# Four 16-column products without a reader at nine places of a two-block transformer kernel

## The chip, the cores and the metric

The kernel runs on one core of one Trainium2 chip, and the chip's other cores do nothing. The metric is device time in microseconds for one execution, from the launch to the last output byte. A core has five engines that run on their own queues and meet only at semaphores: TensorE (PE, matrix products; its weight loads are shown as a row of their own, PEld), VectorE (DVE), ScalarE (ACT), GpSimd (POOL) and SyncE (SP), which here only issues transfers. Products are written to PSUM, a memory of eight banks; everything else lies in SBUF.

## The reference

The reference takes 256 tokens of width 1024 (float32) through a first block of two layers and then a second block of one layer. Cut to what is computed:

```python
# first block, DEPTH = 2
for layer in range(2):
    x = x + 0.5 * swiglu(rmsnorm(x, ffn1_norm[layer]), ffn1_w_gu[layer], ffn1_w_down[layer])
    h = rmsnorm(x, mix_norm[layer])
    y = mixer_gated_deltanet(h, ...) if layer == 0 else mixer_sliding_window_sinks(h, ...)
    x = x + y
    x = x + 0.5 * swiglu(rmsnorm(x, ffn2_norm[layer]), ffn2_w_gu[layer], ffn2_w_down[layer])
x = rmsnorm(x, final_norm)
# second block: 16 meta tokens are put ahead; one mixer (retention + MLA attention, two gates), one swiglu
merged = sigmoid(a_gret) * y_ret + sigmoid(a_gmla) * y_mla
x = x + merged @ w_o
x = x + swiglu(_rmsnorm(x, norm_ffn), w_gate, w_up, w_down)

def rmsnorm(x, w):   # y = x / sqrt(mean(x * x) + eps) * w
def swiglu(h, w_gu, w_down):
    gate, up = split(h @ w_gu)
    return (silu(gate) * up) @ w_down
```

The swiglu width is 2816, so each of the five feed-forward layers ("FFN" below) multiplies by 3 x 1024 x 2816 weights. With the mixers' matrices some 244 MB of weights are read once each.

## The kernel before

The activations stay in SBUF, feature-major: eight tiles of 128 features x 256 tokens (272 in the second block, with the meta tokens). Weights are streamed by `Stream`: SP loads 1 MB chunks into three buffers `raw`, and each chunk is cut into pieces of 512 columns, which ACT copies to `whi` (rounded to fp32r, L355) and DVE completes with the rest `wlo = raw - whi` (L356). Activations are split into `xh` and `xl` in the same way.

A linear layer is `lin` (L373 to L375): for each 128 x 128 weight block three products are added into one PSUM bank, whi by xh, wlo by xh and whi by xl, each with 256 moving columns. So one FFN has 44 x 8 x 3 + 8 x 22 x 3 = 1584 such products, and nearly all of the program on PE is a long run of them. Below, a *stretch* is such a run without another kind of instruction in between, and the *pitch* is the time from the start of one product to the start of the next.

Every layer starts with `opening` (L444). The norm's scale 1/rms is not needed before the first results leave PSUM, so the opening runs the first three banks (jobs a, b, c) on unscaled inputs and slips the scale in between: `rnorm_nat` sums the squares over the features by products with one moving column (L413), DVE and POOL make 1/rms of it (L426, L383), and `row_bcast` spreads it to rows of 128 partitions by two products (L435; float32, which PE runs as two passes each, so four rows in the trace). After these the rest of job c follows. There are eight openings: FFN 10, the DeltaNet mixer (whose job a is 16 columns wide), FFN 20, FFN 11, the window mixer, FFN 21, the retention mixer (272 columns) and FFN 30.

The last mixer ends with attention heads in an order written out by hand (`MLA_PLAN`), whose last entry `w3` is a product of attention weights and values (L1361). Behind it come the two gates (Stream `wga`, 16 banks by `lin`), the products with `wmo`, and the output projection `wo`.

The order of instructions on each engine is made by a list scheduler from the order of the program, priorities and its own cost estimates, so a line may be issued somewhat earlier or later than it is written. PSUM has two pools, `ps` with three banks for `lin` and `pm` with five for everything else.

Of the kernel before, what the change touches and what calls it, by code (L numbers as in the profile page):

```python
# [17 lines left out]
P = 128  # L18
D = 1024
KD = 8  # L20
S = 256
# [200 lines left out]
def kernel(ctx: ExitStack, tc: tile.TileContext, dram: dict, out: bass.AP, dump=None):  # L222
# [26 lines left out]
    pm = ctx.enter_context(tc.tile_pool(name="pm", bufs=5, space=PSUM))  # L249
    uid = [0]  # L250

    def nm(base):
        uid[0] += 1
        return f"{base}_{uid[0]}"

    def sb(at, shape, tag, dt=F32, bufs=None):

        kw = {} if bufs is None else {"bufs": bufs}
        free = int(np.prod(shape[1:]))
        whole = -(-free * 4 // LINE) * LINE // 4  # L260
        if not isinstance(at, Home):
            return at.tile(shape, dt, tag=tag, name=nm(tag), **kw)
        if at.lines is None or whole != free and (dt != F32R or free * 4 < LINE):
            return at.rest.tile(shape, dt, tag=tag, name=nm(tag), **kw)
        if whole == free:
            return at.lines.tile(shape, dt, tag=tag, name=nm(tag), **kw)
        assert len(shape) == 2
        return at.lines.tile([shape[0], whole], dt, tag=tag, name=nm(tag), **kw)[:, :free]

    def bank(pool, shape):  # L270
        return pool.tile(shape, F32, tag="bank", name=nm("bank"))

    def f32(ap):
        return ap.bitcast(F32)

    mm = nc.tensor.matmul
# [90 lines left out]
    def lin(o, st, off, xs, w=P, n=S, ks=None):  # L367

        last = len(xs) - 1
        for k in range(len(xs)) if ks is None else ks:  # L370
            xh, xl = xs[k]
            wh, wl = st.at(off + k * w, w)
            mm(o, wh, xh[:, :n], start=k == 0, stop=False)  # L373
            mm(o, wl, xh[:, :n], start=False, stop=False)  # L374
            mm(o, wh, xl[:, :n], start=False, stop=k == last)  # L375

    def split(src, hi, lo):
        A.copy(hi, src)  # L378
        V.tensor_tensor(lo, src, f32(hi), op=ALU.subtract)  # L379
# [35 lines left out]
    def rnorm_nat(ssq, denom, n=S):  # L415

        nt = (n + P - 1) // P
        b = bank(pm, [P, 512])
        ssq_nat(b, ssq, n)
        v = sb(sp, [P, 4], "rn", bufs=4)  # L420
        if n % P:
            V.memset(v, 1.0)
            V.tensor_scalar(v[:, : nt - 1], b[:, : nt - 1], 1.0 / denom, EPS, op0=ALU.mult, op1=ALU.add)
            V.tensor_scalar(v[: n % P, nt - 1 : nt], b[: n % P, nt - 1 : nt], 1.0 / denom, EPS, op0=ALU.mult, op1=ALU.add)
        else:
            V.tensor_scalar(v[:, :nt], b[:, :nt], 1.0 / denom, EPS, op0=ALU.mult, op1=ALU.add)  # L426
        rsq(v[:, :nt], nt)
        return v

    def row_bcast(v, n=S, tag="r"):  # L430

        b = bank(pm, [P, 512])
        for c in range((n + P - 1) // P):
            m = min(P, n - c * P)
            mm(b[:, c * P : c * P + m], v[:m, c : c + 1].to_broadcast([m, P]), ident[:m, :m], start=True, stop=True)  # L435
        r = sb(sp, [P, ST], tag, bufs=2 if tag == "r" else 1)
        V.tensor_copy(r[:, :n], b[:, :n])
        return r

    def opening(norm, jobs, stats=None, n=S, at=(5, 1)):  # L440


        a, b, c = ((lambda ks, j=j: lin(*j[0], ks=ks, **j[1])) for j in jobs)
        stats = stats or (lambda: rnorm_nat(norm.ssq, D))  # L444
        a(range(KD - 1))
        b(range(at[0]))
        if at[0] < KD - 1:
            rn = stats()
        b(range(at[0], KD - 1))
        a([KD - 1])  # L450
        b([KD - 1])
        if at[0] >= KD - 1:
            rn = stats()
        c(range(at[1]))
        r = row_bcast(rn, n)
        c(range(at[1], KD))
        return r

    def ffn(name, norm, after, scale, hook=None, gu=None, first=None):

        with home(nm("ffn")) as fp:
# [6 lines left out]
            if first:  # L468
                first()
            r = opening(norm, [(pre[i], {}) for i in range(3)], at=(KD - 1, 3) if first else (5, 1))  # L470
            for m in range(KF):
                for i in (2 * m, 2 * m + 1):
                    if i not in pre:
                        pre[i] = proj(i)
                        lin(*pre[i])
                pg, pu = pre.pop(2 * m)[0], pre.pop(2 * m + 1)[0]
                g = sb(fp, [P, S], "ffg", bufs=2)
                V.tensor_tensor(g, pg, r[:, :S], op=ALU.mult)  # L478
                u = sb(fp, [P, S], "ffu", bufs=2)
                V.tensor_tensor(u, pu, r[:, :S], op=ALU.mult)  # L480
                A.activation(g, g, AF.Silu)  # L481
                V.tensor_tensor(u, g, u, op=ALU.mult)  # L482
                ah = sb(fp, [P, S], f"ah{m}", F32R)
                al = sb(fp, [P, S], f"al{m}", F32R)
                split(u, ah, al)
                acts.append((ah, al))
# [9 lines left out]
    def proj_out(st, off, xs, add, after=None):  # L496
        n = len(xs)
        pre = [bank(ps, [P, S]) for d in range(2)]
        for ks in (range(n - 1), [n - 1]):
            for d in range(2):  # L500
                lin(pre[d], st, off + d * n * P, xs, ks=ks)
        for d in range(KD):
            if d < 2:
                pd = pre[d]
            else:
                pd = bank(ps, [P, S])
                lin(pd, st, off + d * n * P, xs)
            add(d, pd)
            if after:
                after(d)  # L510
# [5 lines left out]
    def deltanet(norm, after):  # L516
        with home("gdn") as gp, tc.tile_pool(name="gdr", bufs=1, space=bass.MemoryType.DRAM) as dp:
# [4 lines left out]
            for i in range(2):  # L522
                pre[qk, i] = bank(ps, [P, S])
                jobs.append(((pre[qk, i], qk, i * D, norm.xs), {}))
            r = opening(norm, jobs)

            raw = set(pre)
# [359 lines left out]
            def out_half(q, after=None):  # L887
                OH = sb(gp, [P, 4, S], f"dn{q}", F32R)
                OL = sb(gp, [P, 4, S], f"dt{q}", F32R)
                xs = []  # L890
                for j in range(4):
                    h = 4 * q + j
                    zs = ZS[h]
                    V.tensor_tensor(zs, zs, OT[h // 2][:, (h % 2) * S : (h % 2) * S + S], op=ALU.mult)
                    split(zs, OH[:, j, :], OL[:, j, :])
                    xs.append((OH[:, j, :], OL[:, j, :]))
                proj_out(aout, q * 4 * D, xs, add_x, after)
# [10 lines left out]
    def window(norm, after):  # L908
        with home("swa") as gp:
            st = Stream("bin")  # L910
            QKV = {}
            first = [bank(ps, [P, S]) for j in range(3)]
            r = opening(norm, [((first[j], st, j * D, norm.xs), {}) for j in range(3)])

            def proj(j):
# [57 lines left out]
            def weigh(pr, blk, hf):  # L973
                if not hf:
                    OB[pr, blk] = bank(pm, [P, 4, P])
                ob = OB[pr, blk]
                n = 2 * pr + hf
                for c in range(blk + 1):
                    mm(ob[hf * 64 : hf * 64 + 64, :, :], vn[:, c, n * 64 : n * 64 + 64], PT[pr, blk, hf, c], start=c == 0, stop=c == blk)  # L979
                if hf:  # L980
                    split(ob, OH[pr][:, :, blk * P : blk * P + P], OL[pr][:, :, blk * P : blk * P + P])
# [47 lines left out]
    def retention_mla(norm, stats, finish, dec, after):  # L1029
        xs = norm.xs  # L1030
        Y = [None] * H
        with home("mx") as gp:
            with home("ret") as rp:
                st = Stream("wret")
# [172 lines left out]
            with home("mla") as rp:  # L1207
                str_ = Stream("wro")
                b = bank(pm, [P, 3, 32])
# [26 lines left out]
                b = bank(pm, [P, ST])  # L1236
# [10 lines left out]
                for j in range(4):  # L1247
                    b = bank(ps, [P, ST])
# [11 lines left out]
                for c in range(3):  # L1260
                    m = P if c < 2 else NM
                    b = bank(ps, [P, 512])
                    for k in range(2):
                        wh, wl = stv.at(k * 512, 512)
# [112 lines left out]
                for w in MLA_PLAN.split():  # L1377
                    {"s": scores, "t": turn, "w": weigh, "y": ret_out}[w[0]](int(w[1]))
                st, stm = Stream("wga"), Stream("wmo")
                ME = []  # L1380
                for d in range(KD):
                    ga = []
                    for j in range(2):
                        b = bank(ps, [P, S])
# [5 lines left out]
                    b = bank(ps, [P, S])  # L1390
# [5 lines left out]
                    split(ga[0], m[:, 0, :], m[:, 1, :])  # L1396
                    ME.append((m[:, 0, :], m[:, 1, :]))

            proj_out(Stream("wo"), 0, ME, add_x, after)

# [18 lines left out]
    b = bank(pm, [P, 512])  # L1419
# [81 lines left out]
    def finish():  # L1501
# [3 lines left out]
        if dump:  # L1505
            dump("x4", X[0][:, :S])

    retention_mla(mixn, mix_rms, finish, dec[0], feed("norm_ffn_2"))
    if dump:
        dump("x5", X[0][:, :S])  # L1510
# [13 lines left out]
    b = bank(pm, [P, 512])  # L1524
# [25 lines left out]
```

## Time and profile before

| | |
|---|---|
| Time before, median of 3 runs | 1466.39 us (1466.23 to 1467.72) |
| Profiled execution, its own time | 1458.11 us |
| Its span, first to last instruction | 1456.3 us |
| PE busy with products | 1426.7 us (98%) |
| DVE, ACT, POOL busy | 1106.2, 858.5, 116.3 us |
| Granted TensorE clock, mean | 0.995 of full |
| Instructions on PE | 12318 products, 12318 weight loads |

Every product has a weight load of its own. A matmul is pipelined, so the rows of one stretch overlap: each product is shown as some 0.28 us long, but the next starts 0.11 to 0.12 us after it. The busy share therefore tells little about PE's rate. The rate is read from the starts, or from the number of products in a window of the time line. The profiled execution was 8.28 us shorter than the median of the three runs.

### The profile page before, as it was taken

How to read it: one execution, taken by the hardware profiler on the slowest of the kernel's cores; microseconds unless marked ns; L12 is line 12 of the kernel's file. 1: busy time of each engine (PE TensorE's matmuls, PEld its weight loads, DVE VectorE, ACT ScalarE, POOL GpSimd, SP SyncE). 2: the span in 40 equal slices, each digit the busy share in tenths (PEclk: the TensorE clock that was granted, in tenths of full speed). 3: DMA queues.
4: the chain of work that ended last, by engine and by line, in shares of the span. 5: the costliest groups of instructions: out<-in, count | busy, mean ns of one | idle time of the engine just before them, and what ended most of it. 6: DMA issues, size and time to landing. Idle time of an engine off the chain costs nothing.

```text
span 1456.3 us, 31032 instructions
## 1 busy us (share of the span) xinstructions
PE 1426.7 (98%) x12318; PEld 1396.2 (96%) x12318; DVE 1106.2 (76%) x2340; ACT 858.5 (59%) x1767; POOL 116.3 (8%) x136
## 2 busy tenths in 40 slices
PE   8999999998999999999999999999999999999997
PEld 8999999998999999999998899999999899999997
DVE  6877667896877766777668877788887868777764
ACT  6555558555655555555556665566545766665552
POOL 2000131011200001000010100013001000100000
PEclk9999999999999999999999999999999999999999
DMA  7655443541456555555552455555333425555551
GB/s 253 227 200 197 159 169 116 169 155 44 156 192 203 186 194 199 184 194 203 188 189 88 145 200 182 198 197 180 123 139 109 145 98 200 197 202 192 189 198 59
DMA packets 46369, 248.35 MB, mean 171 GB/s; under 512 B 11408, under 2 KB 16272, under 8 KB 17168
## 3 DMA queue, kind: packets, MB, share of 16 engines
q1 hardware_dynamic: 45680, 245.87, 49.5%
q8 instruction: 97, 1.59, 0.4%
q10 hardware_dynamic: 544, 0.50, 0.1%
q14 instruction: 48, 0.39, 0.1%
HBM read 243.99 MB, written 2.36 MB: 169 GB/s over the span
## 4 chain that ended last, share of the span: by engine, by line
PE 87%; DVE 7%; ACT 3%; DMA 1%; issue 1%; POOL 1%; SPq 0%; DVEq 0%; POOLq 0%; ACTq 0%
PE bank L373 26%; PE bank L375 26%; PE bank L374 26%; DVE wlo L356 2%; ACT whi L355 1%; DVE cv L652 1%; PE bank L979 1%; PE bank L830 1%; PE bank L1331 1%; PE bank L1136 0%; PE bank L1361 0%; DVE xl L395 0%; PE bank L969 0%; POOL rr L383 0%; DMA xt<-xt 0%
## 5 line engine op out<-in xcount | busy, mean ns | idle before, releaser
L356 DVE TENSOR_TENSOR wlo<-raw,whi 128x512 fp32r<-128x512 f32 x922 | 641.6, 700 | 254.2 <-ACT whi L355 252.7
L355 ACT CAST whi<-raw 128x512 fp32r<-128x512 f32 x922 | 565.5, 619 | 430.4 <-PE bank L375 406.1
L373 PE MATMUL bank<-xh,whi 128*128 128x256 f32 (+1 forms) x2488 | 695.1, 279 | 1.7 <-ACT whi L355 1.0
L374 PE MATMUL bank<-xh,wlo 128*128 128x256 f32 (+1 forms) x2488 | 690.8, 278 | 2.0 <-DVE wlo L356 2.0
L375 PE MATMUL bank<-xl,whi 128*128 128x256 f32 (+1 forms) x2488 | 690.4, 278 | 1.0 <-DVE xl L395 0.9
L373 PEld LDWEIGHTS bank<-xh,whi 128*128 128x128 f32 x2488 | 466.8, 188 | 4.0 <-issue 1.8
L374 PEld LDWEIGHTS bank<-xh,wlo 128*128 128x128 f32 x2488 | 467.0, 188 | 3.2 <-DVE wlo L356 2.8
L375 PEld LDWEIGHTS bank<-xl,whi 128*128 128x128 f32 x2488 | 466.6, 188 | 2.1 <-DVE xl L395 1.6
L375 PE MATMUL bank<-al,whi 128*128 128x256 f32 x880 | 242.9, 276 | 0.0
L373 PE MATMUL bank<-ah,whi 128*128 128x256 f32 x880 | 242.9, 276 | 0.0
L374 PE MATMUL bank<-ah,wlo 128*128 128x256 f32 x880 | 242.9, 276 | 0.0
L373 PEld LDWEIGHTS bank<-ah,whi 128*128 128x128 f32 x880 | 165.2, 188 | 0.0
L374 PEld LDWEIGHTS bank<-ah,wlo 128*128 128x128 f32 x880 | 165.2, 188 | 0.0
L375 PEld LDWEIGHTS bank<-al,whi 128*128 128x128 f32 x880 | 165.2, 188 | 0.0
L407 POOL TENSOR_TENSOR ssq<-sq,ssq 128x256 f32<-128x256 f32 (+1 forms) x72 | 62.9, 874 | 1066.3 <-ACT sq L406 1056.7
L378 ACT CAST ah<-ffu 128x256 fp32r<-128x256 f32 x110 | 44.8, 407 | 26.4 <-DVE ffu L482 26.3
L482 DVE TENSOR_TENSOR ffu<-ffg,ffu 128x256 f32<-128x256 f32 x110 | 46.7, 425 | 4.7 <-ACT ffg L481 1.2
L481 ACT ACTIVATE ffg<-ffg 128x256 f32<-128x256 f32 x110 | 45.4, 414 | 4.0 <-DVE ffg L478 3.7
L478 DVE TENSOR_TENSOR ffg<-bank,r 128x256 f32<-128x256 f32 x110 | 46.6, 424 | 0.9 <-PE bank L375 0.8
L480 DVE TENSOR_TENSOR ffu<-bank,r 128x256 f32<-128x256 f32 x110 | 46.6, 424 | 0.1
L379 DVE TENSOR_TENSOR al<-ffu,ah 128x256 fp32r<-128x256 f32 x110 | 46.0, 418 | 0.6 <-ACT ah L378 0.5
L373 PE MATMUL bank<-dec,whi 128*128 128x256 f32 x128 | 36.8, 287 | 0.0
(368 smaller groups left out, 1429.8 us busy)
## 6 DMA issues: line engine op xcount, KB each, us to landing
raw<-gu SPq DMA_DIRECT2D x109, 1024.0 KB, 4.8
raw<-dn SPq DMA_DIRECT2D x55, 1024.0 KB, 4.8
raw<-wret SPq DMA_DIRECT2D x12, 1024.0 KB, 4.8
raw<-aqk SPq DMA_DIRECT2D x8, 1024.0 KB, 4.7
raw<-wga SPq DMA_DIRECT2D x8, 1024.0 KB, 4.8
raw<-bin SPq DMA_DIRECT2D x6, 1024.0 KB, 4.9
raw<-az SPq DMA_DIRECT2D x4, 1024.0 KB, 4.9
raw<-av SPq DMA_DIRECT2D x4, 1024.0 KB, 5.0
```

What stands on the lines that cost most here:

```text
L355: A.copy(hi[:, :n], raw[:, o : o + n])
L356: V.tensor_tensor(lo[:, :n], raw[:, o : o + n], f32(hi[:, :n]), op=ALU.subtract)
L373: mm(o, wh, xh[:, :n], start=k == 0, stop=False)
L374: mm(o, wl, xh[:, :n], start=False, stop=False)
L375: mm(o, wh, xl[:, :n], start=False, stop=k == last)
L378: A.copy(hi, src)
L379: V.tensor_tensor(lo, src, f32(hi), op=ALU.subtract)
L407: G.tensor_tensor(acc[:, :n], q[:, :n], acc[:, :n], op=ALU.add)
L478: V.tensor_tensor(g, pg, r[:, :S], op=ALU.mult)
L480: V.tensor_tensor(u, pu, r[:, :S], op=ALU.mult)
L481: A.activation(g, g, AF.Silu)
L482: V.tensor_tensor(u, g, u, op=ALU.mult)
```

## The change

A new helper `settle` takes one PSUM bank of `pm`, takes the first weight block of a stream, and issues four products of its first 16 columns with the first activation tile. Nothing reads the bank. It is called in `opening` right after `row_bcast`, with the stream and the inputs of job c, and once before the loop over the last mixer's gates. Nothing is removed. The weight piece that it reads is one that the following products read too, so no load and no split is added.

```diff
@@ -374,6 +374,13 @@
             mm(o, wl, xh[:, :n], start=False, stop=False)
             mm(o, wh, xl[:, :n], start=False, stop=k == last)
 
+    def settle(st, off, xs):
+
+        b = bank(pm, [P, 512])
+        wh, _ = st.at(off, P)
+        for i in range(4):
+            mm(b[:16, :S], wh[:, :16], xs[0][0][:, :S], start=True, stop=True)
+
     def split(src, hi, lo):
         A.copy(hi, src)
         V.tensor_tensor(lo, src, f32(hi), op=ALU.subtract)
@@ -453,6 +460,7 @@
             rn = stats()
         c(range(at[1]))
         r = row_bcast(rn, n)
+        settle(*jobs[2][0][1:4])
         c(range(at[1], KD))
         return r
 
@@ -1377,6 +1385,7 @@
                 for w in MLA_PLAN.split():
                     {"s": scores, "t": turn, "w": weigh, "y": ret_out}[w[0]](int(w[1]))
                 st, stm = Stream("wga"), Stream("wmo")
+                settle(st, 0, xs)
                 ME = []
                 for d in range(KD):
                     ga = []
```

In the changed kernel the new products stand on line 382, and the lines behind it are 7 to 9 higher. On PE, at the opening of FFN 20, before the change (bank 5318 is job c's, 5400 that of the rows of 1/rms):

```order
L373 MATMUL bank_5318<-xh_990_5141,whi_5393 128x256
L374 MATMUL bank_5318<-xh_990_5141,wlo_5394 128x256
L375 MATMUL bank_5318<-xl_991_5142,whi_5393 128x256
L435 MATMUL bank_5400<-tabs_81,rn_5376 128x128 x2
L373 MATMUL bank_5318<-xh_993_5148,whi_5393 128x256
L374 MATMUL bank_5318<-xh_993_5148,wlo_5394 128x256
```

The same place on PE in the changed kernel (the bank of the four products is 5415, with 16 rows):

```order
L373 MATMUL bank_5328<-xh_992_5151,whi_5403 128x256
L374 MATMUL bank_5328<-xh_992_5151,wlo_5404 128x256
L375 MATMUL bank_5328<-xl_993_5152,whi_5403 128x256
L442 MATMUL bank_5410<-tabs_81,rn_5386 128x128 x2
L382 MATMUL bank_5415<-xh_992_5151,whi_5403 16x256 x4
L373 MATMUL bank_5328<-xh_995_5158,whi_5403 128x256
L374 MATMUL bank_5328<-xh_995_5158,wlo_5404 128x256
```

The four stand together between the row products and the rest of job c; it is so in seven of the eight openings, and before the gates, behind `w3`. In the first opening, that of FFN 10, PE's order before was:

```order
L413 MATMUL bank_250<-ones_83,ssq_165 128x1 x2
L373 MATMUL bank_164<-xh_12_116,whi_258 128x256
L435 MATMUL bank_271<-tabs_81,rn_253 128x128 x2
L374 MATMUL bank_164<-xh_12_116,wlo_259 128x256
L375 MATMUL bank_164<-xl_13_117,whi_258 128x256
L373 MATMUL bank_164<-xh_16_124,whi_258 128x256
```

and PE's order in the changed kernel's first opening is:

```order
L420 MATMUL bank_250<-ones_83,ssq_165 128x1 x2
L373 MATMUL bank_164<-xh_12_116,whi_258 128x256
L442 MATMUL bank_271<-tabs_81,rn_253 128x128 x2
L382 MATMUL bank_276<-xh_12_116,whi_258 16x256
L374 MATMUL bank_164<-xh_12_116,wlo_259 128x256
L375 MATMUL bank_164<-xl_13_117,whi_258 128x256
L373 MATMUL bank_164<-xh_16_124,whi_258 128x256
L374 MATMUL bank_164<-xh_16_124,wlo_259 128x256
L375 MATMUL bank_164<-xl_17_125,whi_258 128x256
L373 MATMUL bank_164<-xh_18_128,whi_258 128x256
L374 MATMUL bank_164<-xh_18_128,wlo_259 128x256
L375 MATMUL bank_164<-xl_19_129,whi_258 128x256
L382 MATMUL bank_276<-xh_12_116,whi_258 16x256 x3
```

Here the four are apart: one directly behind the row products, three after eight products of job c. On DVE and ACT a few weight splits (L355, L356) stand one to four places later or earlier around the openings; POOL and SP keep their order.

## Rows read from the trace of the kernel before

**Rows 1.** The page: span, engines' busy time, chain that ended last by engine

```profile
span 1456.3 us, 31032 instructions
PE 1426.7 (98%) x12318; PEld 1396.2 (96%) x12318; DVE 1106.2 (76%) x2340; ACT 858.5 (59%) x1767; POOL 116.3 (8%) x136
PE 87%; DVE 7%; ACT 3%; DMA 1%; issue 1%; POOL 1%; SPq 0%; DVEq 0%; POOLq 0%; ACTq 0%
```

**Rows 2.** Waits of PE: releaser, us in total, times, longest

```profile
PE bank L592 <- DVE g L585: 2.7, 1, 2.7
PE bank L435 <- POOL rn L383: 2.2, 2, 1.2
```

**Rows 3.** Windows: us, busy (xcount) of PE, PEld, DVE, ACT, POOL; clock, DMA, GB/s

```profile
40.00:198.00 158.00, 158.00 (x1397) 157.59 (x1396) 113.45 (x206) 90.17 (x169) 6.59 (x9) 1.00 0.58 198
392.00:568.00 176.00, 176.00 (x1556) 176.00 (x1555) 128.74 (x234) 101.66 (x189) 6.11 (x7) 1.00 0.57 193
...
1190.00:1268.00 78.00, 78.00 (x691) 78.00 (x690) 63.58 (x121) 50.35 (x98) 5.02 (x7) 1.00 0.55 190
1273.00:1445.00 172.00, 172.00 (x1520) 172.00 (x1520) 121.47 (x223) 94.06 (x172) 5.25 (x6) 1.00 0.51 172
```

**Rows 4.** Time line of PE, FFN 10's opening: start, us, operation, count, idle before

```profile
19.06 0.71 PE L435 MATMUL bank<-tabs,rn 128*128 128x128 f32 x4 [1.21 <-POOL rn L383]
19.53 0.36 PE L374 MATMUL bank<-xh,wlo 128*128 128x256 f32 x1
19.73 0.28 PE L375 MATMUL bank<-xl,whi 128*128 128x256 f32 x1
...
30.68 0.28 PE L375 MATMUL bank<-xl,whi 128*128 128x256 f32 x1
...
31.68 0.39 PE L374 MATMUL bank<-xh,wlo 128*128 128x256 f32 x1 [0.34 <-DVE wlo L356]
```

**Rows 5.** Time line of PE, FFN 20's opening

```profile
389.09 0.28 PE L374 MATMUL bank<-xh,wlo 128*128 128x256 f32 x1
...
390.62 0.28 PE L375 MATMUL bank<-xl,whi 128*128 128x256 f32 x1
390.74 0.61 PE L435 MATMUL bank<-tabs,rn 128*128 128x128 f32 x4
391.10 0.37 PE L373 MATMUL bank<-xh,whi 128*128 128x256 f32 x1
391.31 0.28 PE L374 MATMUL bank<-xh,wlo 128*128 128x256 f32 x1
391.42 0.28 PE L375 MATMUL bank<-xl,whi 128*128 128x256 f32 x1
```

**Rows 6.** Time line of PE, end of DeltaNet's 16-column job a

```profile
195.45 0.28 PE L375 MATMUL bank<-xl,whi 128*16 128x256 f32 x1
...
197.15 0.28 PE L375 MATMUL bank<-xl,whi 128*16 128x256 f32 x1
197.26 0.28 PE L373 MATMUL bank<-xh,whi 128*128 128x256 f32 x1
```

**Rows 7.** Time line of the weight loads (PEld) at the same place

```profile
197.04 0.09 PEld L375 LDWEIGHTS bank<-xl,whi 128*16 128x16 f32 x1
197.15 0.19 PEld L373 LDWEIGHTS bank<-xh,whi 128*128 128x128 f32 x1
```

**Rows 8.** Time line of PE, the last three 16-column products of that job

```profile
200.12 0.28 PE L373 MATMUL bank<-xh,whi 128*16 128x256 f32 x1
...
200.46 0.28 PE L373 MATMUL bank<-xh,whi 128*128 128x256 f32 x1
...
201.05 0.28 PE L375 MATMUL bank<-xl,whi 128*128 128x256 f32 x1
```

**Rows 9.** Time line of PE, first products of the last mixer's gates

```profile
1188.88 0.38 PE L373 MATMUL bank<-xh,whi 128*128 128x256 f32 x1
1189.10 0.29 PE L374 MATMUL bank<-xh,wlo 128*128 128x256 f32 x1
```

## The prediction

> **What bounds the kernel now.** I read the page first: PE is busy 98% of the span, and the chain of waits that ended last runs 87% through PE [rows 1]. The list of waits then tells where PE stands still: its longest single wait is 2.7 us, in the DeltaNet mixer, for a DVE result, and the row products L435 wait 1.2 us once [rows 2]. Everything else is PE at its own rate, so whatever is put on PE counts in full, unless it falls ahead of one of those waits.
>
> Since PE's busy share hides its rate, I read the rate from the windows. In a long stretch there are 1556 products in 176 us [rows 3]; two or three of them only reach in at the edge, because a product is shown for 0.28 us and the window counts what overlaps it, so the pitch is 176/1553.5 = 113.3 ns. The other five long stretches give the same: three are in [rows 3], and two that repeat the pattern, in FFN 11 and FFN 21, have x1555 in 176 us and x1520 in 172 us.
>
> The time line shows a second pitch. In FFN 10 the products from 19.73 to 30.68 are 93 steps in 10.95 us, 117.7 ns [rows 4]. In FFN 20 the 13 steps from 389.09 to 390.62, behind the sums of squares, take 1.53 us, again 117.7 ns, and behind the row products the stretch has 113.3 [rows 5, 3]. So the same instruction runs at one of two pitches, 4.4 ns or 3.9% apart, and it keeps the pitch until something interrupts the stretch: at 31.68 a wait for wlo ends the slow one of FFN 10, and the 158 us from 40 on are fast [rows 4, 3]. Which pitch a stretch gets is settled in its first few products. In this execution all six long stretches are fast; the slow ones are short, and only FFN 10's stands behind row products.
>
> **The change part by part.**
>
> *The added products.* Nine places by four products, 36 in all. A product with 16 weight columns and 256 moving columns costs the stretch as much as one with 128: the 15 steps from 195.45 to 197.15 take 1.70 us, 113.3 ns [rows 6]. Its weight load is shown as 0.09 us against 0.19 us [rows 7], but the load is not what the pitch waits for there. So 36 x 0.1133 = 4.08 us as an upper bound at the fast pitch, and 36 x 0.1177 = 4.24 us at the slow one.
>
> *What they take over.* A stretch does not start at its pitch. In FFN 20 the second product starts 0.21 us after the first (391.10 to 391.31) and the third 0.11 us after that [rows 5]; at the gates the second starts 0.22 us after the first [rows 9]. That is some 0.1 us above the pitch, which the added products would pay in place of the real ones. Since their loads are shorter, the delay may be gone: then a place costs 0.45 - 0.10 = 0.35 us. If the delay only moves, it costs 0.45 us. No row shows a stretch that begins with 16-column products, so I take the middle, 0.40 us per place, and keep 0.35 and 0.45 as ends.
>
> *What hides them.* In the DeltaNet opening the products that follow run into the 2.7 us wait for DVE [rows 2], and DVE is fed by the rows of 1/rms, which stand ahead of the added products; 0.4 us vanish there. If that cover were gone they would cost their 0.40 us. At the other eight places no wait of PE follows that does not itself hang on PE's progress, so 8 x 0.40 = 3.2 us stand on the path.
>
> *What they give.* FFN 10's opening is the one place where a slow pitch follows row products. If the one added product directly behind them gives a fast start, the 72 products up to the point where DVE, ACT and then PE run into the next wait (19.73 to 28.2 us) gain 72 x 4.4 ns = 0.32 us; that the stretch later stalls for whi and wlo is chained to PE's own progress. If it stays slow, nothing is gained. I take the gain.
>
> *Moved splits, the bank.* A weight split on ACT or DVE that stands up to four places later is ready long before its use: DVE is busy 128.74 of 176 us and ACT 101.66 [rows 3], and eight pieces of 12 products each are ahead, 8 x 12 x 0.113 = 10.9 us. Cost nothing; without that cover a split would show as one wait of some 0.6 us. The extra bank of the five in `pm` is taken when the earlier readers are done: ahead of the openings lie only the sums and the rows, ahead of the gates 24-product jobs. Nothing is queued behind a new wait.
>
> *Sum.* 3.2 - 0.3 = 2.9 us on the profiled execution: span 1456.3 + 2.9 = 1459.2, own time 1458.11 + 2.9 = 1461.0. With the ends, 8 x 0.35 - 0.3 = 2.5 and 9 x 0.45 + 0.2 = 4.3 us. The median of the runs, 1466.39, is 8.28 us above the profiled execution. If that distance holds, the changed kernel comes to 1466.39 + 2.9 = 1469.3 us, its own range being 1468.2 to 1470.9.
>
> In the stretches above the trace has 113.3 or 117.7 ns per product. [...]
>
> **The rivals.**
>
> *A: the runs without a profile have slow stretches, and the added products end them.* For it: 8.28 us between the profiled execution and the median is 0.57%, while the three runs lie within 0.1% of each other. At 4.4 ns each it is 8.28/0.0044 = 1880 products, a little more than the length of one FFN (1584), or FFN 10 with the gates. FFN 10 escapes its slow pitch in the profile only by a stall [rows 4], and the gates start behind attention work that itself waits. Against it: in the trace the stretch behind the row products is fast in every FFN but the first, so there it looks built in, not a chance; and a distance that has to do with how an execution is timed would not go away. Time if all of it goes: 1466.39 - 8.28 + 2.9 = 1461.0 us. If only one FFN is freed, 1466.39 - 1584 x 0.0044 + 2.9 = 1462.3.
>
> *B: only a short part is freed,* the gates with their outputs (16 x 24 + 8 x 12 + 8 x 24 = 672 products, 3.0 us) or FFN 10's beginning. Time: 1466.39 - 3.0 + 2.9 = 1466.3 us.
>
> *C: the added products tip stretches into the slow pitch.* The mechanism lies at the four FFN openings behind the first, which have the same instructions and so likely the same fate: a fast start there is what the row products give now, and the 16-column products take their place as the last thing before the stretch. The price is 1520 to 1556 products by 4.4 ns, 6.8 us for each, the point from which it decides is the second or third real product. For it: three 16-column products in a slow stretch did not make it fast, since the five steps behind them, 200.46 to 201.05, take 0.59 us, 118 ns [rows 8]. Against it: 16-column products run at the fast pitch for 15 steps and hand over to full ones without a break [rows 6, 3], and with their shorter loads they should reach it at once. Time with one FFN slow: 1469.3 + 6.8 = 1476 us; with four, 1469.3 + 27 = 1497 us. In FFN 10, where the four stand apart, it would be the same 6.5 us if the later stall no longer ends it.
>
> *D: the change doesn't do what it says.* The products have no reader; if they were dropped in the build, nothing would be left but moved splits. The order shows them on PE, so this has no chance of its own.
>
> **How the numbers follow.** The forecast gets 0.50, A 0.25, B 0.12, C 0.13. The predicted time is that of the forecast, 1469.3 us. A measurement of this kernel tells about 0.2%, 2.9 us, from no change, so faster means under 1463.5 and slower over 1469.3: the forecast sits on the border, and I split it 0.27 no change, 0.23 slower, a little more below because the delay at a stretch's start is likely saved. A is faster in nearly all of its cases (0.24), B no change with a little faster (0.10 and 0.02), C slower unless small (0.12); the hundredth left of A and of C counts as no change. That makes 0.26 faster, 0.39 the same, 0.35 slower. The range takes in A down to 1460.5 and part of C up to 1474; beyond it lie C's whole FFNs, about 0.12, and a few hundredths below.
>
> **What would show it.** In the profile after, the added line should have 36 rows at 16 columns, with starts 0.11 us apart, and each place should push the next stage by 0.35 to 0.45 us, except DeltaNet. The windows of the six long stretches should hold as many products as before (some 884 in 100 us); 849 in 100 us means the slow pitch, and decides for C. FFN 10's products behind its row products should start 0.113 us apart instead of 0.118. A cannot be seen in a profile alone: it shows if the profiled execution becomes longer and the median shorter, so that their distance of 8.28 us shrinks. The prediction is wrong if the median leaves 1468.2 to 1470.9, and its first assumption, that the runs have the pitches of the profile, is what I trust least.

## The result, and the profile after

The changed kernel takes 1486.54 us (median of 4 runs, 1482.05 to 1492.61) against 1466.36 us (median of 4, 1466.23 to 1467.72) before: ratio 1.0149, 95% interval 1.011 to 1.0187. It is slower by 1.5%, the interval leaves no change out, and it lies above the range of the prediction. The profiled execution took 1482.05 us. It is the shortest of the four; no profile shows what made the other three 1.5 to 10.6 us longer.

The page of the changed kernel, to be read against [rows 1]: span, busy time of the engines, chain that ended last by engine.

```profile
span 1480.3 us, 31106 instructions
PE 1450.8 (98%) x12354; PEld 1419.6 (96%) x12354; DVE 1110.9 (75%) x2340; ACT 858.7 (58%) x1767; POOL 116.5 (8%) x136
PE 89%; DVE 5%; ACT 2%; issue 1%; DMA 1%; POOL 1%; SPq 0%; DVEq 0%; POOLq 0%; ACTq 0%
```

The span grew by 24.0 us, and PE's busy time by 24.1 us with 36 more products. Nothing here is a new wait: PE itself needs longer. The windows of the long stretches say where. They are, in order, FFN 10, FFN 20, FFN 11, FFN 21, the gates and FFN 30; the columns are those of [rows 3].

```profile
40.00:198.00 158.00, 158.00 (x1396) 157.59 (x1396) 113.92 (x207) 90.49 (x169) 6.59 (x9) 1.00 0.58 199
393.00:569.00 176.00, 176.00 (x1496) 176.00 (x1496) 125.24 (x227) 98.24 (x183) 5.25 (x6) 1.00 0.55 186
582.00:757.00 175.00, 175.00 (x1547) 175.00 (x1546) 127.48 (x231) 101.44 (x188) 6.08 (x7) 1.00 0.57 194
847.00:1019.00 172.00, 172.00 (x1462) 172.00 (x1462) 135.22 (x256) 104.44 (x201) 10.16 (x10) 1.00 0.55 185
1206.00:1284.00 78.00, 78.00 (x691) 78.00 (x690) 63.42 (x120) 50.33 (x98) 4.72 (x7) 1.00 0.55 190
1290.00:1462.00 172.00, 172.00 (x1463) 172.00 (x1462) 121.95 (x220) 92.24 (x170) 4.39 (x5) 1.00 0.50 172
```

FFN 10, FFN 11 and the gates hold as many products as before. FFN 20 has 1496 in 176 us where [rows 3] has 1556; FFN 30 has 1463 in 172 us in place of 1520, and FFN 21 1462. With the two or three products at the edge taken off, that is 172/1460.5 = 117.8 ns against 172/1517.5 = 113.3 ns. Three FFNs run at the slow pitch from the first product to the last, at a granted clock of 1.00 (2.4 GHz) as before, so the clock isn't it. The short stretch of the window mixer's opening (761.1 to 780.4 us) is slow too.

The sum: 1568 + 1532 + 1532 products in the FFNs and 164 in the window mixer are 4796, by 4.44 ns 21.3 us; the added products with 0.44 us at each of the eight open places (below) 3.5 us. That is 24.8 us for the 24.0 measured. FFN by FFN it holds: from one opening's sums to the next, FFN 20 grew by 7.4 us, FFN 11 by 0.4, the window mixer by 1.2, FFN 21 by 7.2 and FFN 30 by 7.3. The rest agrees only in total: FFN 10's beginning, fast now (below), gave 0.3 us back, and the retention mixer came out 1.1 us shorter where the sum has 0.4 longer, against some 1 us lost in small parts elsewhere. That was not followed up.

The time line of PE in FFN 30's opening shows where the pitch is set. L420 are the sums of squares, L442 the rows of 1/rms, L382 the added products; columns as in [rows 5].

```profile
1285.55 0.50 PE L420 MATMUL bank<-ones,ssq 128*128 128x1 f32 x4
...
1286.11 0.28 PE L374 MATMUL bank<-xh,wlo 128*128 128x256 f32 x1
...
1287.64 0.28 PE L375 MATMUL bank<-xl,whi 128*128 128x256 f32 x1
1287.76 0.61 PE L442 MATMUL bank<-tabs,rn 128*128 128x128 f32 x4
1288.12 0.71 PE L382 MATMUL bank<-xh,whi 128*16 128x256 f32 x4
1288.67 0.28 PE L373 MATMUL bank<-xh,whi 128*128 128x256 f32 x1
...
1289.14 0.28 PE L374 MATMUL bank<-xh,wlo 128*128 128x256 f32 x1
```

The sums leave the 13 steps between 1286.11 and 1287.64 slow (1.53 us, 117.7 ns), just as in [rows 5]. There the row products alone turned the slow pitch into the fast one. Here the four added products stand behind them, and the 4 steps from 1288.67 to 1289.14 take 0.47 us, 117.5 ns: the slow pitch stays, for 1532 products. In FFN 11, which stands behind a slow FFN 20, the same instructions gave the fast one:

```profile
579.25 0.61 PE L442 MATMUL bank<-tabs,rn 128*128 128x128 f32 x4
579.62 0.70 PE L382 MATMUL bank<-xh,whi 128*16 128x256 f32 x4
580.16 0.28 PE L373 MATMUL bank<-xh,whi 128*128 128x256 f32 x1
580.27 0.28 PE L374 MATMUL bank<-xh,wlo 128*128 128x256 f32 x1
...
580.95 0.28 PE L374 MATMUL bank<-xh,wlo 128*128 128x256 f32 x1
```

Six steps from 580.27 to 580.95 are 0.68 us, 113.3 ns. From the row products to the second real one it is 1.02 us here and 0.57 us in [rows 5]: 0.45 us for four added products. By the raw starts, up to the 21st real product of FFN 11, it is 0.44.

### The profile page after: what moved, and what is told of

Read it like the earlier page. It is cut to its first block, busy times and chain, and to the rows that moved or that the text cites. A ratio compares the mean times of both kernels' runs of the same rounds, so it can differ in the third digit from the quotient of the medians.

```text
span 1480.3 us, 31106 instructions
## 1 busy us (share of the span) xinstructions
PE 1450.8 (98%) x12354; PEld 1419.6 (96%) x12354; DVE 1110.9 (75%) x2340; ACT 858.7 (58%) x1767; POOL 116.5 (8%) x136
## 4 chain that ended last, share of the span: by engine, by line
PE 89%; DVE 5%; ACT 2%; issue 1%; DMA 1%; POOL 1%; SPq 0%; DVEq 0%; POOLq 0%; ACTq 0%
PE bank L373 27%; PE bank L375 27%; PE bank L374 27%; DVE wlo L356 1%; PE bank L987 1%; PE bank L838 1%; PE bank L1339 0%; PE bank L1144 0%; ACT whi L355 0%; PE bank L1369 0%; DVE xl L402 0%; DMA xt<-xt 0%; PE bank L977 0%; DVE cv L660 0%; PE bank L1357 0%
## 5 line engine op out<-in xcount | busy, mean ns | idle before, releaser
L356 DVE TENSOR_TENSOR wlo<-raw,whi 128x512 fp32r<-128x512 f32 x922 | 640.8, 699 | 267.4 <-ACT whi L355 265.3
L355 ACT CAST whi<-raw 128x512 fp32r<-128x512 f32 x922 | 565.0, 618 | 447.4 <-PE bank L375 418.4
```

What stands on the lines that cost most here:

```text
L355: A.copy(hi[:, :n], raw[:, o : o + n])
L356: V.tensor_tensor(lo[:, :n], raw[:, o : o + n], f32(hi[:, :n]), op=ALU.subtract)
```

## The experiments

**What changed from run to run.** The prediction's base was a profiled execution 8.28 us below the median of the runs. The first question was what that gap is, so the kernel before was run again, unchanged.

> The kernel before once more, unchanged. Theory (the entry of a stretch decides its pitch): time follows the number of products at 117.8 ns instead of 113.3 ns. If the profiled execution is again near 1458 us, all six long stretches are at 113.3 ns; an execution near 1466 us must show one long stretch (some 1,500 products, 6.8 us) or FFN 10 in the slow pitch. Rival (the 8.28 us between the profiled execution and the timed runs belong to how an execution is timed): 1466 us with all long stretches at 113.3 ns.

Measured: 1471.3 us (1464.05 to 1478.59, 10 runs), ratio 0.9993, 0.9965 to 1.002. The profile took 1471.8 us. Its windows of FFN 20 and FFN 21:

```profile
393.00:569.00 176.00, 176.00 (x1497) 176.00 (x1496) 125.00 (x225) 97.75 (x183) 5.20 (x6) 1.00 0.55 187
844.00:1016.00 172.00, 172.00 (x1462) 172.00 (x1462) 135.60 (x256) 105.57 (x201) 10.11 (x10) 1.00 0.55 185
```

Both FFNs are slow, in the very kernel whose first profile had them fast: 1567 + 1531 products by 4.44 ns are 13.8 us, and the profiled spans differ by 13.7 (1470.0 against 1456.3). The time line of this execution at FFN 20's opening:

```profile
389.63 0.28 PE L374 MATMUL bank<-xh,wlo 128*128 128x256 f32 x1
...
390.42 0.28 PE L375 MATMUL bank<-xl,whi 128*128 128x256 f32 x1
390.54 0.60 PE L435 MATMUL bank<-tabs,rn 128*128 128x128 f32 x4
...
391.10 0.28 PE L374 MATMUL bank<-xh,wlo 128*128 128x256 f32 x1
...
391.69 0.28 PE L373 MATMUL bank<-xh,whi 128*128 128x256 f32 x1
```

Ahead of the row products the 7 steps from 389.63 to 390.42 take 0.79 us, 113 ns; behind them the 5 steps from 391.10 to 391.69 take 0.59 us, 118 ns. In [rows 5] it was slow ahead and fast behind. So the row products turn the pitch over, whichever it is: where nothing is added around them, every slow piece of 15 products became fast (35 of 35 in the FFNs and the window mixer, all profiles taken together), and 4 of 4 fast pieces became slow (two here, two in the profile of the kernel with one changed place, below). What changes from run to run is the piece between sums and rows, and only in FFN 20 and FFN 21: there the sums wait for POOL and start 0.24 to 0.25 us after the product ahead of them (rows of before are shown below); in FFN 11, the window mixer and FFN 30 they follow at 0.12 us and leave the piece slow every time. Of the 12 pieces behind such a wait, in the six profiles that have the sums where they were, ten are fast and two slow, both in the first profile of the kernel before. The same 0.24 us gave either, so nothing that was read here tells which it will be, and "chance" below means no more than that. Among these profiles the first is the rare case.

This changes what the first comparison means. FFN 20 and FFN 21 are slow in this execution too, with nothing added, and against it the changed kernel is only 10.3 us longer (1480.3 against 1470.0). FFN 30 (6.8), the window mixer (0.7) and the places (3.5), less FFN 10's beginning (0.3), make 10.7.

The pitch may not be all of the scatter. Of the 25 runs of the unchanged kernel that stand beside this one, the 13 with a mean granted clock of 0.990 to 0.992 have a median of 1473.96 us and the 12 with 0.994 to 0.997 one of 1470.20 us. In the profiles the low clock lies outside the six long stretches, which all have 1.00. How much of the scatter is the clock's was not separated.

**The added products ahead of the row products.** The change with the two calls swapped in `opening`:

```diff
-        r = row_bcast(rn, n)
         settle(*jobs[2][0][1:4])
+        r = row_bcast(rn, n)
```

> The four products stand ahead of the row products in the openings, so that each stretch starts behind the row products as before the change; the ones at the gates stay. Theory (entry): the FFN stretches are fast again, time 1466 + 4 = 1470 us, within 2 us. Rival (the added products, their bank or the moved splits cost the time wherever they stand): 1482 to 1492 us as with the change.

Measured: 1490.35 us (1487.44 to 1497.1, 4 runs), ratio 1.0118, 1.0075 to 1.016. Its profile (1497.1 us) has FFN 11 slow, the stretch that the change left fast:

```profile
584.00:759.00 175.00, 175.00 (x1489) 174.91 (x1488) 123.83 (x226) 96.55 (x179) 5.43 (x6) 1.00 0.55 186
```

and FFN 10, FFN 20, the window mixer, FFN 21 and FFN 30 as well. The time expected was missed by 20 us: which instruction stands last ahead of the stretch does not settle it alone.

**All 128 columns.** The change with the full weight block in the four products:

```diff
-            mm(b[:16, :S], wh[:, :16], xs[0][0][:, :S], start=True, stop=True)
+            mm(b[:, :S], wh, xs[0][0][:, :S], start=True, stop=True)
```

> The change with all 128 weight columns in the added products instead of 16. Theory (entry behind the row products decides, 16-column loads upset it): the stretch starts as before, 36 more products at 113.3 ns, 1466 + 4 = 1470 us. Rival (any shift of the start time re-rolls the pitch of each stretch, whatever the width): some long stretches slow, 1476 us or more, and not the same ones as with 16 columns.

Measured: 1477.95 us (1468.85 to 1483.22, 10 runs), ratio 1.0031, 1.0007 to 1.0056. FFN 20 and FFN 21 are slow in its profile, as in that of the kernel before from the same chip, and FFN 30, at 1292 to 1464 us, is fast:

```profile
1292.00:1464.00 172.00, 172.00 (x1520) 172.00 (x1519) 121.43 (x223) 93.40 (x172) 5.24 (x6) 1.00 0.51 172
```

Four products of full width cost about what they take, 8 x 0.45 us = 3.6 us against 4.6 measured by the ratio (1.0 to 8.2 by its interval). Four products of 16 columns keep FFN 30 and the window mixer slow; four of 128 columns do not.

**One place alone.** The kernel before with the four products in FFN 30's opening only:

```diff
         r = row_bcast(rn, n)
+        if jobs[2][0][1].ap is dram["gu30"]:
+            settle(*jobs[2][0][1:4])
```

> The four products only in the opening of FFN 30, the last; everything ahead of it is the kernel before. Theory (entry): FFN 30's 1,532 products run at 117.8 ns as in the profile of the change, so 1466 + 0.3 + 6.8 = 1473 us; if its start falls right, 1466.7 us. Rival (cost spread over all places): 1466 + 24/9 = 1469 us, with FFN 30 at 113.3 ns.

Measured: 1479.37 us (1474.78 to 1484.82, 10 runs), ratio 1.0056, 1.0025 to 1.0088; against the median of the unchanged kernel on the same chip (1472.75 us, 25 runs) 6.6 us more, where the interval of the ratio allows 3.7 to 13. FFN 30 in its profile:

```profile
1288.00:1460.00 172.00, 172.00 (x1463) 172.00 (x1462) 122.10 (x220) 91.73 (x170) 4.47 (x6) 1.00 0.50 171
```

One stretch of 1532 products by 4.44 ns is 6.8 us, and the four products there cost 0.4 us. That is the cost of one such place, shown by itself.

**The wait of the sums taken away.** If chance enters where the sums wait for POOL, sums that are issued later must take it out. In FFN 20 and FFN 21 they are put one input tile later (and the row products one, too), in the kernel before:

```diff
-            r = opening(..., at=(KD - 1, 3) if first else (5, 1))
+            r = opening(..., at=(KD - 1, 3) if first else (6, 2) if name in ("20", "21") else (5, 1))
```

> The kernel before, with the sums of squares and the row products of FFN 20 and FFN 21 three products later each (at=(6,2) in place of (5,1)), so that PE no longer waits for POOL at the sums. Theory (a chain: without a wait the 15 products between the sums and the row products are always slow, and behind slow ones the row products always give a fast stretch; only a wait at the sums makes it chance): all five FFNs at 113.3 ns, profiled execution 1458 to 1461 us, median 1458 to 1463 us, spread below that of the kernel before. Rival (each stretch is chance by itself): median as before, 1466 to 1473 us, with one or two long stretches slow.

Measured: 1459.74 us (1455.48 to 1466.94, 10 runs), ratio 0.9927, 0.9895 to 0.9958, against a kernel before with 1470.07 us (22 runs, 1456.04 to 1481.19). First the kernel before at FFN 20: POOL's last sum of squares, then PE's sums behind the last product.

```profile
387.62 0.75 POOL L407 TENSOR_TENSOR ssq<-sq,ssq 128x256 f32<-128x256 f32 x1 [1.61 <-ACT sq L406]
```

```profile
388.17 0.28 PE L375 MATMUL bank<-xl,whi 128*128 128x256 f32 x1
388.42 0.61 PE L413 MATMUL bank<-ones,ssq 128*128 128x1 f32 x4
```

POOL ends at 388.37, the sums start 0.05 us later, 0.25 us behind the last product. With the later sums:

```profile
395.87 0.73 POOL L407 TENSOR_TENSOR ssq<-sq,ssq 128x256 f32<-128x256 f32 x1 [1.61 <-ACT sq L406]
```

```profile
396.76 0.28 PE L375 MATMUL bank<-xl,whi 128*128 128x256 f32 x1
396.88 0.50 PE L413 MATMUL bank<-ones,ssq 128*128 128x1 f32 x4
```

POOL is done at 396.60, and the sums follow at the stretch's own distance, 0.12 us. The windows of FFN 10 and FFN 20 (FFN 21 has x1520 in 172 us):

```profile
40.00:198.00 158.00, 158.00 (x1344) 158.00 (x1343) 111.67 (x201) 87.67 (x163) 5.20 (x6) 1.00 0.56 191
401.00:577.00 176.00, 176.00 (x1555) 176.00 (x1554) 127.83 (x232) 101.20 (x190) 6.11 (x7) 1.00 0.57 194
```

FFN 20 and FFN 21 are fast, here and in all six later profiles that have the later sums without four added products at these two places. FFN 10 is slow in this one; five of the ten runs lie at 1455.5 to 1456.6 us and five at 1462.9 to 1466.9, which is what the 1438 products of its slow stretch by 4.44 ns, 6.4 us, would make of it. That this is FFN 10's own chance (it stalls for weight pieces some 13 us after its row products) fits, but was not tried. The clock can have a part in it too: in this profile the products from 20 to 22 us run at a granted clock of 0.50 (1.2 GHz), 0.21 us apart, where the first profile has 1.00.

**The change with the later sums.**

> The change with the same later sums in FFN 20 and FFN 21. Theory (behind slow products and a row product, four 16-column products give a slow stretch where the stretch ahead of the sums was fast): FFN 20, the window mixer, FFN 21 and FFN 30 slow, FFN 11 fast; 1458 + 3 + 21 = 1482 us, near no spread. Rival (the change's loss came from the wait at the sums alone): 1462 us, with all long stretches fast.

Measured: 1482.85 us (1477.19 to 1490.07, 10 runs), ratio 1.0113, 1.0076 to 1.0151. FFN 20, FFN 11, FFN 21 and FFN 30 in its profile:

```profile
389.00:565.00 176.00, 176.00 (x1497) 176.00 (x1496) 125.37 (x228) 97.88 (x182) 5.22 (x6) 1.00 0.55 186
578.00:753.00 175.00, 175.00 (x1547) 175.00 (x1546) 127.36 (x231) 101.66 (x189) 6.07 (x7) 1.00 0.57 194
843.00:1015.00 172.00, 172.00 (x1463) 172.00 (x1462) 135.33 (x256) 105.64 (x201) 10.14 (x10) 1.00 0.55 185
1286.00:1458.00 172.00, 172.00 (x1462) 172.00 (x1462) 121.81 (x220) 92.09 (x170) 4.39 (x5) 1.00 0.50 172
```

The wait is gone, and the change is as slow as ever: slow, fast, slow, slow, as in the change itself. So the wait brings the chance into the kernel before, and the four products give the changed one its slow pitch where no wait does.

**The number of products.** The kernel before with the later sums, and one, eight, four, two or three 16-column products in FFN 30's opening alone:

```diff
+            for i in range(1):   # in the others 8, 4, 2 or 3
```

> The later sums, and one 16-column product in FFN 30's opening alone. Theory (16-column products keep the alignment of the first one, their number does not matter): FFN 30 slow, 1459 + 0.1 + 6.8 = 1466 us. Rival (their number or the added time decides): FFN 30 fast, 1459 us.

> The later sums, and eight 16-column products in FFN 30's opening alone. Theory (their number does not matter): FFN 30 slow, 1459 + 0.8 + 6.8 = 1466.6 us. Rival (more of them settle to the fast pitch): FFN 30 fast, 1460 us.

> The kernel before with the later sums, and four 16-column products in FFN 30's opening alone; it differs from the kernels with one and with eight of them there only in the number. Theory (the number of added products sets the pitch of the stretch behind them, and four give the slow one here): the window 1,520 products long in FFN 30 is at 117.7 ns, x1461 to x1463 in 172 us in place of x1520, all other long stretches behind FFN 10 fast; time 1455.5 + 6.8 + 0.2 = 1462.5 us, or 1469 to 1474 in runs in which FFN 10 is slow too. Rival (the slow FFN 30 of the change came from where the earlier stretches left the stream, not from the count): FFN 30 fast at 113.3 ns, 1455.7 to 1456.5 us.

> As the one with four, but with two. One left FFN 30 fast and four made it slow in the change. Theory (each added product moves the stream by a step, so that the outcome changes with the count, and not only once): no value is named by it for two; fast gives 1455.7 us and slow 1462.5 us (FFN 10's chance adds up to 7). Rival (only the shortness of the last weight load ahead of the stretch matters): as with one, fast, and then four must be fast too.

> As the one with four, but with three. Theory (a step per product): if the outcome alternates with the count, three is unlike two and unlike four, that is fast at 113.3 ns, 1456 us; if it has a period of three or more, three can be either. Rival (a threshold: few products leave the row products' turn to fast as it is, more than some number undo it): two and three are on one side each, with no return, and eight being fast speaks against it already.

Measured: one 1455.58 us (1455.11 to 1455.91, 4 runs), ratio 0.9884, 0.9843 to 0.9926; eight 1458.31 us (1456.2 to 1463.6, 7 runs), ratio 0.9928, 0.9891 to 0.9966; four 1466.45 us (1462.9 to 1477.72, 10 runs), ratio 0.997, 0.9939 to 1.0001; two and three one run each, 1464.18 us with FFN 10 slow and 1465.47 us with FFN 10 fast. FFN 30's window in the profiles, first with one:

```profile
1271.00:1443.00 172.00, 172.00 (x1520) 172.00 (x1519) 121.00 (x222) 93.86 (x172) 5.25 (x6) 1.00 0.51 172
```

with four:

```profile
1275.00:1447.00 172.00, 172.00 (x1462) 172.00 (x1462) 121.98 (x220) 91.71 (x169) 5.22 (x6) 1.00 0.50 171
```

and with eight:

```profile
1276.00:1448.00 172.00, 172.00 (x1520) 172.00 (x1520) 120.61 (x220) 92.43 (x170) 5.25 (x6) 1.00 0.50 172
```

With two the window of 172 us in FFN 30 has x1519, with three x1463. In the order one, two, three, four, eight that is fast, fast, slow, slow, fast. The idea that the kind of the products matters and not their number fell. So did a threshold, since the pitch returns with eight, and a turn with every single product, since one and two agree. Four behave as in the change in every profile. The lowest runs put the price of a slow FFN 30 at 1462.9 - 1455.1 = 7.8 us, 6.8 of it the pitch and 0.3 the three more products; the other 0.7 us were not followed up, and the two sets come from different chips.

Three profiles have a case that the kernel before did not show. Where FFN 10 is slow, the first 21 products of the DeltaNet mixer's job a, 16 columns each, stand behind a slow stretch. In the profile of the later sums:

```profile
201.49 0.28 PE L374 MATMUL bank<-ah,wlo 128*128 128x256 f32 x1
...
202.08 0.28 PE L373 MATMUL bank<-xh,whi 128*16 128x256 f32 x1
...
202.43 0.28 PE L373 MATMUL bank<-xh,whi 128*16 128x256 f32 x1
...
204.47 0.28 PE L373 MATMUL bank<-xh,whi 128*128 128x256 f32 x1
```

The 5 steps up to the first of them take 0.59 us, 118 ns, and the next three 0.35 us, 117 ns; from the fourth of them on the 18 steps take 2.04 us, 113.3 ns, and the full products behind them keep that. So a longer row of 16-column products comes to the fast pitch by itself, also in the profiles of the swapped calls and of the two products, while three in [rows 8] left a slow stretch slow. That goes with eight being fast and three and four slow; it does not explain one and two.

**One product per place.** The change with the later sums and `range(1)`:

> The change with one 16-column product per place in place of four, and the later sums in FFN 20 and 21. Theory (one product leaves the stretch as the row products alone would, as it did in FFN 30): FFN 20, FFN 11, the window mixer, FFN 21, the gates and FFN 30 all at 113.3 ns, time 1455.5 + 8 x 0.1 = 1456.3 us where FFN 10 is fast and 1463 where it is slow. Rival (16-column products behind row products turn stretches slow whatever their number, FFN 30 with one was an exception): two or more of the five long stretches slow, 1469 us and more.

Measured: 1463.19 us (1459.02 to 1471.17, 10 runs), ratio 0.9937, 0.9906 to 0.9968. The gates and FFN 30 in its profile:

```profile
1190.00:1268.00 78.00, 78.00 (x665) 78.00 (x664) 63.03 (x119) 48.86 (x95) 4.49 (x6) 1.00 0.55 190
1275.00:1447.00 172.00, 172.00 (x1520) 172.00 (x1520) 121.17 (x222) 94.23 (x172) 5.24 (x6) 1.00 0.51 172
```

All FFNs and the window mixer are fast, as expected. The gates are slow, 665 products in 78 us, which was not expected: 707 by 4.44 ns are 3.1 us, and the lowest run is 3.2 us above the 1455.8 us that one product in one place, plus seven places by 0.1 us, would give. The single product gains time nowhere. The faster kernels here are faster by the later sums.

## Why the prediction was wrong

**The added products.** Right: 36 rows of 16 columns, 0.44 us at an opening in front of a fast stretch, where 0.40 was taken and 0.45 kept as an end. The delay at a stretch's start moved to the added products and was not saved.

**What hides them.** Right: the 2.7 us wait of the DeltaNet mixer [rows 2] is shorter by the 0.4 us that were to vanish there, and the product behind it starts 10.3 us after the row products in both profiles (201.17 to 211.44, 201.60 to 211.92). The list of PE's waits in the changed kernel, columns as in [rows 2] (the L592 of before is L600 here):

```profile
PE bank L600 <- issue: 2.3, 1, 2.3
```

**What they give.** The number came out, the reason is not shown. FFN 10's first stretch is fast, 26 steps from 27.73 to 30.67 us in 2.94 us, 113.1 ns, where [rows 4] has 117.7:

```profile
27.73 0.28 PE L373 MATMUL bank<-xh,whi 128*128 128x256 f32 x1
...
30.67 0.28 PE L375 MATMUL bank<-xl,whi 128*128 128x256 f32 x1
```

But the kernel with one product in FFN 30 alone, which adds nothing here, has it fast as well, 93 steps in 10.55 us, 113.4 ns:

```profile
19.14 0.29 PE L375 MATMUL bank<-xl,whi 128*128 128x256 f32 x1
...
29.69 0.28 PE L375 MATMUL bank<-xl,whi 128*128 128x256 f32 x1
```

Of the profiles with nothing added in FFN 10 and a granted clock of 1.00 there, three have it fast (one place alone, one, two) and four slow (both of the kernel before, three, four). Both that have the four products as in the change have it fast. So it varies by itself, and two cases are too few to credit the added product; the 0.3 us may be luck.

**What they take over.** This step failed. The prediction held that only the delay at a stretch's start was at stake, and set against rival C that with their shorter loads the stretches behind the added products "should reach it at once". They do reach a pitch at once, but in FFN 20, FFN 21, FFN 30 and the window mixer it is the slow one. The argument drew on the 15 products of 16 columns in [rows 6], which run inside a stretch that is already fast, and so say nothing on how one begins. The row that spoke of it, [rows 8], where three such products left a slow stretch slow, was read the right way and then outweighed. Rival C was the outcome, with its price right (6.8 us for an FFN). Its reason was not: it lay in the 16-column products being "the last thing before the stretch", and the swapped calls left the stretches slow with the row products last, while one, two and eight products in that place left FFN 30 fast. Its count was not either: three FFNs and the window mixer came out slow, and "the same instructions and so likely the same fate" is wrong for FFN 11. Both profiles that show this have a slow FFN 20 ahead of it, which may be what changes the outcome; four products in FFN 11 behind a fast FFN 20 were not tried. And for FFN 20 and FFN 21 the added products are not needed: where the piece ahead of the rows is fast, as in the changed kernel's profile, the row products alone leave them slow.

**The sum.** "If that distance holds" was the second assumption to fail. The 8.28 us were no fixed offset between a profiled run and the others: profiled again, the kernel took 1471.8 us in a set with a median of 1471.3. It has two chances, FFN 20 and FFN 21, each 7 us, with more from FFN 10, and the first profiled execution was one with none of them lost. That the forecast was built on it was bad luck. What was slow in the three runs at 1466 us no profile shows. Nor does a measurement tell 0.2% from no change, as the prediction had it from three runs: sets of 10 runs give intervals of 0.25 to 0.4% to either side. And its own range did not follow from its ends: 2.5 and 4.3 us make 1468.9 to 1470.7, not 1468.2 to 1470.9. Rival A had this half right, that other runs have slow stretches; it went wrong in what would end them. The change does end most of the chance, in the wrong direction: with four products FFN 20 and FFN 21 came out slow whether the piece ahead of the rows was fast (the changed kernel) or slow (with the later sums). In the three later sets of runs the unchanged kernel's medians were 1472.75, 1470.07 and 1471.65 us, so the 1.5% of the first comparison, made against four runs at 1466 to 1468 us, may be more than the change usually costs; against these medians the 1486.54 us are 0.9 to 1.1% more.

**Open.** What in the machine has two pitches was not found, nor why one, two and eight products leave FFN 30 fast and three and four slow, nor why one made the gates slow. What makes the piece behind a waiting sum fast or slow is open too. FFN 10's chance was seen (slow in the profiles of the swapped calls, of the later sums and of the kernel with two products), and its cause was not tried.

## What to carry to other kernels

Read the rate of a long product stream from the starts, in several executions: a stream that is 98% busy can run at two rates, and what stands at its start can decide which. Where the runs of a kernel scatter, look for a short wait just ahead of a long stretch, and compare the granted clocks of the runs; taking 0.13 us of waiting away from two places was worth 0.7% here. An edit that puts "harmless" instructions at the start of such a stretch has to be priced at the whole stretch, and tried place by place.

## What the runs showed of the hardware

Products with 256 moving columns and a weight load each go at 113.3 or at 117.8 ns, both at a granted clock of 1.00, and keep it over 1560 products. In the FFNs and the window mixer of these 14 profiles the pitch follows from the instructions ahead as long as the sums do not wait. The sums (two products of one column, four rows in the trace), 0.11 to 0.12 us behind the product ahead, left the 15 products behind them slow in 58 of 58 openings. The row products then turned that to fast wherever nothing was added around them, 35 of 35. Four 16-column products behind the row products undid that turn in 8 of 8 stretches whose predecessor was fast and in neither of 2 whose predecessor was slow; both of these are FFN 11. Behind the four in the DeltaNet opening, with its 16-column job a, the products came out fast in both kernels that have them there (the change, and the change with the later sums). Where the sums waited, 0.07 to 0.13 us longer, the piece was fast in 10 cases and slow in 2.
